# Two more column groups of a modulation product (3 and 4 of layer 1) summed on VectorE instead of on TensorE

## The chip, the core and the metric

The kernel runs on one core of a Trainium2 chip. The metric is the device time of one execution in microseconds (us), here the median of three runs. A profiled execution gives the trace that the rows below are read from; its times count from the start of its span.

## The reference, cut to what matters

Two layers work on 256 latent and 256 context tokens of width 2048. In each layer the conditioning vectors give a shift, a scale and a gate for every channel, which is a product of a small matrix (2 rows: latent and context) with a weight matrix of 2048 x 6144:

```
cond_x = silu(c); cond_c = silu(c_ctx)
sh, sc, gt = split(cond @ ada_w[i] + ada_b[i], 3)
u = modulate(rms_norm(h, pre_g[i]), sh, sc)
out = mixer_i(u)          # layer 0: convolution and Fourier; layer 1: attention and state space
h = h + gt * rms_norm(out, post_g[i])
```

All arithmetic is fp32. The modulation of layer 1 depends on the inputs alone, so it can be computed at any time before the input of layer 1 is formed.

## The kernel before

**Weights.** Every weight block of a projection is 512 KB: 2 x 128 rows by 512 columns. `load_w` fetches it into a tile with the tag raw (4 buffers) and splits it into wh (rounded, ScalarE, L73) and wl (the rest, VectorE, L76), of which there are 3 buffers each. Each product is then three matmuls. `next_w` keeps three blocks ahead (`fill_w(3)`, L313 is its DMA).

**Groups and turns.** `group` runs over the 8 weight blocks of a projection. After each block it calls a step function, here called a turn, which hands small pieces of other work to the scheduler at this place of the program. In layer 0 the groups with turns are, in order: five input groups of 8 turns (convolution values and gates, Fourier inputs), the Fourier gates 0 to 3 (8), the Fourier gates 4 to 7 (8), one convolution gate block alone (`nb=1`, `step_odd`: 4 turns in 8 weight blocks, which are 128 KB each here), the last convolution gates (8), and three of the four column blocks of the output product (8 each). That makes 92 turns. The fourth column block runs in two halves (`ao`), each followed by `mid_chain`, which ends layer 0 and gives the input of layer 1. `u1_pair` then forms that input, two channel blocks at a time, with the modulation.

**The modulation in the background.** It is cut into 12 column groups q of 512 columns for each layer; q of 0 to 7 hold scale and shift. Layer 0's first eight are done in a prologue, and the gates of layer 1 elsewhere. The others are done in the turns, by two queues:

- `ada_bg` holds `ada_steps`: per group 8 loads of 512 KB into raw (L359), 16 matmuls of the conditioning with the raw tile into E (L143, four at a time), a copy, and four transposes (ept, L128). It is eight steps per group, and one step is taken in every turn.
- `pool_bg` holds `ada_vec`: per group 8 loads of 512 KB into raw (L381), each with two row blocks of 128. For both conditioning vectors each row block is scaled and added to a sum pa: the first on ScalarE (L385), all others on VectorE (L387). At the end two matmuls with ones add up the partitions (Ep, L392), and four transposes bring the result into place (ept, L399). Each load is one step and the sum is the ninth; the finish falls into the step after it. The two sums have one buffer each.

`pool_bg` is stepped in two turns of three, and only from the moment that the sixth group is through:

```
def step_ada():
    turns[0] += 1
    if turns[1] and turns[0] % 3 < 2:
        run(pool_bg)
    run(ada_bg)
```

What is left of both queues after the third column block of the output product is issued at once, before the fourth:

```
pump(1e9)
run(ada_bg, 1e9)
run(pool_bg, 1e9)
out0_open(3)
```

**Order.** The program is ordered by a scheduler that goes by program order among what is ready on each engine. Engines run their instructions in the order that it fixed. SyncE issues all loads.

Of the kernel before, what the change touches and what calls it, by code (L numbers as in the profile page):

```python
# [40 lines left out]
def tile_backbone(ctx: ExitStack, tc: tile.TileContext, a):  # L41
# [77 lines left out]
    def ada_copy(E):  # L119
        es = scr.tile([P, 512], F32, tag="t512", name="es")  # L120
        S.activation(es, E, AF.Copy)
        return es

    def ada_finish(psp, l, q, es, tag="ps"):

        pt = psp.tile([P, 4, P], F32, tag=tag, name="ept")
        for b in range(4):
            T.transpose(pt[:, b, :], es[:, b * P:(b + 1) * P], ident)  # L128
        V.tensor_reduce(
            ada[l][:, 4 * q:4 * q + 4, :],  # L130
            pt.rearrange("p b (g m) -> p b m g", g=4)[:, :, 0:2, :],
            axis=AX.X, op=ALU.add,
        )
        lo = COLS["adab"][0] + 48 * l + 4 * q
        V.tensor_tensor(
            ada[l][:, 4 * q:4 * q + 4, :], ada[l][:, 4 * q:4 * q + 4, :],
            cols[:, lo:lo + 4].rearrange("p (b o) -> p b o", o=1).to_broadcast([P, 4, 2]),
            ALU.add,
        )

    def ada_mm(E, kt, raw):
        g = kt % 4
        T.matmul(E[32 * g:32 * g + 32, :], condS[:, kt, :], raw,  # L143
                 start=(kt < 4), stop=(kt >= 12), skip_group_check=True)
# [207 lines left out]
    def ada_steps(l, qs):  # L352
        for q in qs:
            E = epool[0].tile([P, 512], F32, tag=epool[1], name="E")
            for kq in range(4):
                ws = []
                for i in range(2):
                    w = wpool.tile([P, 2, 512], F32, tag="raw", name="raw", bufs=4)
                    nc.sync.dma_start(w, a["ada%d" % l][q, kq][:, 2 * i:2 * i + 2, :])  # L359
                    ws.append(w)  # L360
                    if i == 0:
                        yield
                for j in range(4):
                    ada_mm(E, 4 * kq + j, ws[j // 2][:, j % 2, :])
                if kq < 3:
                    yield
            es = ada_copy(E)
            yield
            ada_finish(epool[0], l, q, es, epool[1])
            ada_done(l, (q,))  # L370

    def ada_vec(l, qs, nm, pool):

        accs = []
        for i, q in enumerate(qs):
            accs += [pool.tile([P, 512], F32, tag="pa%d" % (i * nm + m), name="pa")
                     for m in range(nm)]
            for kp in range(8):
                w = wpool.tile([P, 2, 512], F32, tag="raw", name="raw", bufs=4)
                k0 = 2 * (kp % 2)  # L380
                nc.sync.dma_start(w, a["ada%d" % l][q, kp // 2][:, k0:k0 + 2, :])  # L381
                for kt, m in ((2 * kp + j, m) for j in range(2) for m in range(nm)):
                    acc, wj, c = accs[i * nm + m], w[:, kt % 2, :], condS[:, kt, m:m + 1]
                    if kt == 0:
                        S.activation(acc, wj, AF.Copy, scale=c)  # L385
                    else:
                        V.scalar_tensor_tensor(acc, wj, c, acc, ALU.mult, ALU.add)  # L387
                yield
        n = 32 * len(accs)
        E = psp.tile([P, 512], F32, tag="ps", name="Ep")  # L390
        for g, acc in enumerate(accs):
            T.matmul(E[32 * g:32 * g + 32, :], ones[:, 0:32], acc, start=True, stop=True,  # L392
                     skip_group_check=True)
        es = scr.tile([P, 512], F32, tag="t512", name="es")
        S.activation(es[0:n], E[0:n], AF.Copy)
        yield
        pt = psp.tile([P, 4, n], F32, tag="ps", name="ept")
        for b in range(4):
            T.transpose(pt[:, b, :], es[0:n, b * P:(b + 1) * P], ident[0:n, 0:n])  # L399
        for i, q in enumerate(qs):  # L400
            lo = COLS["adab"][0] + 48 * l + 4 * q
            V.tensor_tensor(
                ada[l][:, 4 * q:4 * q + 4, 0:nm],
                pt.rearrange("p b (q m r) -> p q r b m", q=len(qs), m=nm)[:, i, 0],
                cols[:, lo:lo + 4].rearrange("p (b o) -> p b o", o=1).to_broadcast([P, 4, nm]),
                ALU.add)
        ada_done(l, qs)
# [34 lines left out]
    def ada_done(l, qs):  # L442
        for q in qs:
            if q < 8:
                mod_cols(l, q)
            else:
                gates[l] += 1
                if gates[l] == 4:
                    gate_rows(l, *epool)
                    cond_row(*epool)  # L450
# [9 lines left out]
    ada_bg, pool_bg = [], []  # L460
# [49 lines left out]
    l0 = lay0.enter_context(tc.tile_pool(name="l0", side="right", reuse_waits="tile", bufs=1))  # L510
# [260 lines left out]
    utok = lambda kt, t: (uh[kt][:, t * P:(t + 1) * P], ul[kt][:, t * P:(t + 1) * P])  # L771
    kts = list(range(KT))
    for l, qs in ((0, range(8, 12)), (1, range(8))):
        ada_bg.append(ada_steps(l, [q for q in qs if (l, q) not in ((1, 5), (1, 6), (1, 7))]))
        pool_bg += [ada_vec(l, (q,), 2, l0) for q in qs if (l, q) in ((1, 5), (1, 6), (1, 7))]

    def step0():
        step_ada()
# [547 lines left out]
    qs = P ** -0.5  # L1326
# [233 lines left out]
```

## Time and profile before

| what | value |
|---|---|
| median of 3 runs | 1532.35 us (1530.88 to 1534.11) |
| profiled execution | 1529.52 us, of which its span is 1527.5 us |
| TensorE busy | 1467.2 us (96%) |
| VectorE busy | 1041.7 us (68%) |
| ScalarE busy | 568.2 us (37%) |
| mean granted clock of TensorE | 0.993 |

PE is TensorE's matmuls, PEld its weight loads, DVE VectorE, ACT ScalarE and SPq SyncE's queue of DMAs. L76 is line 76 of the kernel. A row of a timeline has the start, the duration, the engine, the line, the operation, output and inputs, the count of merged instructions, and in brackets the idle time before with what ended it.

### The profile page before, as it was taken

How to read it: one execution, taken by the hardware profiler on the slowest of the kernel's cores; microseconds unless marked ns; L12 is line 12 of the kernel's file. 1: busy time of each engine (PE TensorE's matmuls, PEld its weight loads, DVE VectorE, ACT ScalarE, POOL GpSimd, SP SyncE). 2: the span in 40 equal slices, each digit the busy share in tenths (PEclk: the TensorE clock that was granted, in tenths of full speed). 3: DMA queues.
4: the chain of work that ended last, by engine and by line, in shares of the span. 5: the costliest groups of instructions: out<-in, count | busy, mean ns of one | idle time of the engine just before them, and what ended most of it. 6: DMA issues, size and time to landing. Idle time of an engine off the chain costs nothing.

```text
span 1527.5 us, 22085 instructions
## 1 busy us (share of the span) xinstructions
PE 1467.2 (96%) x8261; PEld 1186.9 (78%) x8261; DVE 1041.7 (68%) x2427; ACT 568.2 (37%) x1113; POOL 183.6 (12%) x179
## 2 busy tenths in 40 slices
PE   3999999999999999999998999999999999999996
PEld 1556777777777766778778999897888979889885
DVE  5234999999863654655367725779799897746645
ACT  4232111122223323232256624454554545324542
POOL 0000000010130000000000100335144354000000
PEclk9999999999999999999999999999999999999998
DMA  9975444454615566664364534224344544536653
GB/s 387 365 307 226 143 164 166 164 168 142 207 45 186 204 207 221 204 204 160 103 223 170 169 108 145 83 101 149 132 160 133 176 143 145 201 117 209 227 189 114
DMA packets 75261, 269.89 MB, mean 177 GB/s; under 512 B 8401, under 2 KB 12049, under 8 KB 70417
## 3 DMA queue, kind: packets, MB, share of 16 engines
q1 hardware_dynamic: 75152, 268.47, 51.1%
q8 instruction: 65, 1.06, 0.3%
q14 instruction: 44, 0.35, 0.1%
HBM read 264.21 MB, written 4.23 MB: 176 GB/s over the span
## 4 chain that ended last, share of the span: by engine, by line
PE 79%; DVE 15%; DMA 3%; issue 2%; ACT 1%; SPq 0%; DVEq 0%; ACTq 0%
PE acc L495 35%; PE kv L495 12%; PE ao L495 8%; PE E L143 4%; DVE wl L76 3%; PE aq L495 2%; PE ag L495 2%; PE acc L204 2%; PE acc L205 2%; PE adg L495 1%; PE acc L203 1%; DMA raw<-in_ada1g_dram 1%; PE po L1296 1%; PE Sc L1267 1%; DVE acc L245 1%
## 5 line engine op out<-in xcount | busy, mean ns | idle before, releaser
L73 ACT ACTIVATE wh<-raw 128x1024 fp32r<-128x1024 f32 (+1 forms) x264 | 274.4, 1040 | 600.4 <-PE acc L495 267.8
L76 DVE TENSOR_TENSOR wl<-raw,wh 128x1024 fp32r<-128x1024 f32 (+1 forms) x264 | 322.4, 1224 | 202.9 <-ACT wh L73 202.0
L530 DVE SCALAR_TENSOR_TENSOR cv<-ain,cw,cv 128x512 f32<-128x512 f32 x240 | 170.4, 750 | 0.0
L495 PE MATMUL acc<-uh,wh 128*128 128x512 f32 x400 | 161.7, 404 | 2.5 <-ACT wh L73 2.0
L495 PE MATMUL acc<-uh,wl 128*128 128x512 f32 x400 | 158.0, 399 | 2.0 <-DVE wl L76 2.0
L495 PE MATMUL acc<-ul,wh 128*128 128x512 f32 x400 | 158.5, 396 | 0.0
L495 PE MATMUL kv<-wh,uh 128*128 128x256 f32 x384 | 109.8, 286 | 2.5 <-DVE sg L1341 2.5
L387 DVE SCALAR_TENSOR_TENSOR pa<-raw,condS,pa 128x512 f32<-128x512 f32 x90 | 63.1, 747 | 69.3 <-DMA raw<-in_ada_dram 62.6
L495 PE MATMUL kv<-wl,uh 128*128 128x256 f32 x384 | 109.4, 285 | 0.0
L495 PE MATMUL kv<-wh,ul 128*128 128x256 f32 x384 | 108.6, 283 | 0.0
L495 PEld LDWEIGHTS acc<-uh,wh 128*128 128x128 f32 x400 | 75.6, 189 | 41.5 <-ACT wh L73 11.0
L495 PEld LDWEIGHTS acc<-uh,wl 128*128 128x128 f32 x400 | 75.9, 190 | 22.2 <-DVE wl L76 2.8
L495 PE MATMUL kv<-uh,wh 128*128 128x512 f32 (+1 forms) x224 | 86.4, 388 | 5.9 <-ACT uh L920 5.9
L495 PEld LDWEIGHTS acc<-ul,wh 128*128 128x128 f32 x400 | 75.6, 189 | 17.0 <-issue 0.8
L495 PE MATMUL kv<-ul,wh 128*128 128x512 f32 (+1 forms) x224 | 82.7, 370 | 0.0
L495 PE MATMUL kv<-uh,wl 128*128 128x512 f32 (+1 forms) x224 | 82.2, 369 | 0.0
L495 PEld LDWEIGHTS kv<-wh,uh 128*128 128x128 f32 x384 | 72.7, 189 | 6.2 <-DVE sg L1341 3.4
L495 PE MATMUL acc<-wh,uh 128*128 128x512 f32 x192 | 76.7, 401 | 0.0
L495 PE MATMUL acc<-wl,uh 128*128 128x512 f32 x192 | 76.6, 399 | 0.0
L495 PE MATMUL acc<-wh,ul 128*128 128x512 f32 x192 | 76.3, 397 | 0.0
L495 PE MATMUL acc<-wh,mh 128*128 128x512 f32 x192 | 76.0, 398 | 0.0
L495 PE MATMUL acc<-wl,mh 128*128 128x512 f32 x192 | 75.5, 393 | 0.0
(405 smaller groups left out, 3328.1 us busy)
## 6 DMA issues: line engine op xcount, KB each, us to landing
raw<-in_w_dram SPq DMA_DIRECT2D x184, 512.0 KB, 3.5
raw<-in_ada_dram SPq DMA_DIRECT2D x96, 512.0 KB, 4.7
raw<-in_wo_dram SPq DMA_DIRECT2D x72, 512.0 KB, 3.2
aw<-in_ada_dram SPq DMA_DIRECT2D x32, 1024.0 KB, 7.1
raw<-in_ada1g_dram SPq DMA_DIRECT2D x32, 512.0 KB, 3.3
w<-in_w0a_dram SPq DMA_DIRECT2D x8, 896.0 KB, 6.8
h<-in_h_dram SPq DMA_DIRECT2D x4, 1024.0 KB, 8.0
h0t<-in_h0t_dram SPq DMA_DIRECT2D x16, 256.0 KB, 4.3
```

Source lines behind the costliest of these rows:

```text
L73: S.activation(hi, src, AF.Copy)
L76: slo.tensor_tensor(lo, src, hi.bitcast(F32), ALU.subtract)
L143: T.matmul(E[32 * g:32 * g + 32, :], condS[:, kt, :], raw, start=(kt < 4), stop=(kt >= 12), skip_group_check=True)
L203: T.matmul(ps, wh, xh, start=start, stop=False)
L204: T.matmul(ps, wh, xl, start=False, stop=False)
L205: T.matmul(ps, wl, xh, start=False, stop=stop)
L245: V.tensor_tensor(acc, acc, sq, ALU.add)
L387: V.scalar_tensor_tensor(acc, wj, c, acc, ALU.mult, ALU.add)
L495: T.matmul(out, lt, rt, start=st and m == 0, stop=en and m == 2, skip_group_check=True)
L530: ins = V.scalar_tensor_tensor(o, x[:, :, k:k + L], cw05[:, ch, k:k + 1], o, ALU.mult, ALU.add)
L1267: T.matmul(Sc, qT[:, i, t * P:(t + 1) * P], kT[:, i, :], start=True, stop=True)
L1296: T.matmul(po, vT[:, k, i * P:(i + 1) * P], U_["PT"][:, k, :], start=k == 0, stop=k == 3)
```

## The change

Column groups 3 and 4 of layer 1 are taken from the list of `ada_steps` and put into that of `ada_vec`, ahead of groups 5, 6 and 7, which were there before. Nothing else changes.

```diff
 for l, qs in ((0, range(8, 12)), (1, range(8))):
-    ada_bg.append(ada_steps(l, [q for q in qs if (l, q) not in ((1, 5), (1, 6), (1, 7))]))
-    pool_bg += [ada_vec(l, (q,), 2, l0) for q in qs if (l, q) in ((1, 5), (1, 6), (1, 7))]
+    ada_bg.append(ada_steps(l, [q for q in qs if (l, q) not in ((1, 3), (1, 4), (1, 5), (1, 6), (1, 7))]))
+    pool_bg += [ada_vec(l, (q,), 2, l0) for q in qs if (l, q) in ((1, 3), (1, 4), (1, 5), (1, 6), (1, 7))]
```

## Rows read from the trace of the kernel before

**Rows 1.** The page: busy time of each engine, share, instructions.

```profile
PE 1467.2 (96%) x8261; PEld 1186.9 (78%) x8261; DVE 1041.7 (68%) x2427; ACT 568.2 (37%) x1113; POOL 183.6 (12%) x179
```

**Rows 2.** Waits of TensorE, 480 to 840 us: total, times, longest.

```profile
PE kv L495 <- ACT uh L920: 5.9, 1, 5.9
PE acc L495 <- ACT wh L73: 2.0, 3, 1.0
```

**Rows 3.** The chain that ended last, 600 to 770 us: start, us, what.

```profile
607.35 0.99 PE E L143 x8
...
644.23 1.14 PE E L143 x8
...
651.14 0.51 PE ept L128 x4
...
736.58 0.98 PE Ep L392 x4
...
748.92 0.39 PE ept L399 x4
749.31 11.36 PE acc L495 x48
```

**Rows 4.** Timeline of SyncE's DMA queue, 480 to 840 us.

```profile
482.11 0.80 SPq L855 DMA_DIRECT2D h0t<-in_h0t_dram  x2
...
645.89 0.33 SPq L313 DMA_DIRECT2D raw<-in_wo_dram  x1
647.02 0.33 SPq L381 DMA_DIRECT2D raw<-in_ada_dram  x1
647.44 8.75 SPq L313 DMA_DIRECT2D raw<-in_wo_dram  x3
657.19 0.33 SPq L381 DMA_DIRECT2D raw<-in_ada_dram  x1
...
713.23 0.33 SPq L381 DMA_DIRECT2D raw<-in_ada_dram  x1
```

**Rows 5.** Busy time by window, the group of one block.

```profile
core 0: us, PE busy (x) PEld busy (x) DVE busy (x) ACT busy (x) POOL busy (x), PEclk, DMA share, GB/s
549.30:566.60 17.30, 15.26 (x62) 9.01 (x60) 7.56 (x16) 4.57 (x10) 0.00 (x0) 1.00 0.71 229
```

**Rows 6.** Busy time by window of the instructions on E alone.

```profile
549.30:566.60 17.30, 3.16 (x12) 0.43 (x12) 0.00 (x0) 1.00 0.71 229
570.00:760.00 190.00, 8.71 (x52) 1.43 (x52) 1.16 (x2) 1.00 0.55 181
```

**Rows 7.** The chain that ended last, 545 to 570 us.

```profile
549.20 5.01 DMA raw<-in_w0t_dram
```

**Rows 8.** Tile pa: ns (min/median/max), first and last start.

```profile
L387 DVE SCALAR_TENSOR_TENSOR pa<-raw,condS,pa x90: 740/746/754, 490.1 to 720.5; 128x512 f32<-128x512 f32 x90
...
L385 ACT ACTIVATE pa<-raw,condS x6: 708/718/726, 489.3 to 664.9; 128x512 f32<-128x512 f32 x6
```

**Rows 9.** Timeline of VectorE, 640 to 665 us.

```profile
643.12 2.74 DVE L387 SCALAR_TENSOR_TENSOR pa<-raw,condS,pa 128x512 f32<-128x512 f32 x4 [4.55 <-DMA raw<-in_ada_dram]
```

**Rows 10.** Timeline of VectorE, 715 to 832 us.

```profile
726.55 1.23 DVE L76 TENSOR_TENSOR wl<-raw,wh 128x1024 fp32r<-128x1024 f32 x1 [1.73 <-ACT wh L73]
...
737.71 1.23 DVE L76 TENSOR_TENSOR wl<-raw,wh 128x1024 fp32r<-128x1024 f32 x1 [4.34 <-ACT wh L73]
744.47 1.23 DVE L76 TENSOR_TENSOR wl<-raw,wh 128x1024 fp32r<-128x1024 f32 x1 [5.54 <-ACT wh L73]
...
750.05 1.23 DVE L76 TENSOR_TENSOR wl<-raw,wh 128x1024 fp32r<-128x1024 f32 x1 [0.34 <-ACT wh L73]
...
761.49 0.69 DVE L874 TENSOR_TENSOR oG<-acc,gt 128x512 f32<-128x512 f32 x1 [0.77 <-ACT jk L873]
```

**Rows 11.** DMA issues, 700 to 790 us: count, size, median us to landing.

```profile
raw<-in_wo_dram SPq DMA_DIRECT2D x22, 512.0 KB, 3.2
raw<-in_ada_dram SPq DMA_DIRECT2D x2, 512.0 KB, 4.4
```

**Rows 12.** Busy time by window after the wait in the middle.

```profile
819.50:825.00 5.50, 5.36 (x24) 5.34 (x25) 4.33 (x16) 5.50 (x16) 0.00 (x0) 0.50 0.01 5
```

## The prediction, written before the change was run

> **What bounds the kernel now.** I read the shares of the engines first: TensorE is busy 96% of the span [rows 1]. Then who waited for whom on TensorE around the stretch that the change touches, 480 to 840 us: its two longest waits add up to 7.9 us, one of 5.9 us behind the middle chain and 2.0 us in three pieces [rows 2]. So in this stretch TensorE sets the time, and any TensorE work taken out is won, as long as nothing new makes it wait. Third, the chain that ended last, 600 to 770 us: it is an unbroken run of TensorE work, in which the summed modulation appears as blocks of 1 us (E, and ept behind it) between weight products [rows 3]. VectorE is not the bound here, but it shares one thing with TensorE's supply: the four buffers with the tag raw. Every weight block of `load_w` and every modulation block passes through them, and SyncE issues them in the order of the program [rows 4].
>
> **What is removed.** Groups 3 and 4 leave `ada_steps`. Each is 16 matmuls, four at a time, and four transposes. On the chain four matmuls take 0.99 to 1.14 us and the transposes 0.51 us [rows 3]. Two groups: 8 x 1.02 + 2 x 0.5 = about 9 us. This counts them as they overlap on the chain; the busy time of all records of the two groups, 3.16 + 8.71 us [rows 6], holds their tails too and is the upper bound, 12. The Trainium skill (TensorE: Matmul & The Clock Gate, "Part 3: Packing small matmuls — row/col tiling") says the same: matmuls with 32 output rows that go to different column groups of the array run side by side, 2.38 times as fast for three of them. So this rule speaks against the change: what it takes away was already cheap. The trace agrees (four fp32 matmuls in 0.99 us); run one after another they would be, by the same row's factor as an estimate, some 20 us instead of 8, and the sum below would be +4 or +5.
>
> The two groups are also the last two of `ada_bg`. That queue gives one step per turn and eight steps per group, nine groups now, so it ends with turn 72; after the change with turn 56. Turns 57 to 60 are the group with one block (the gate of channel block 7), where each weight block carries only 6 matmuls; it lasts 17.3 us with TensorE busy 15.3 [rows 5], and the chain runs there through DMAs into raw buffers (5.0 us the first, [rows 7]). Four of the modulation loads vanish from it. I take the 2 us of idle time as won; bounds 0 and 2.7 (17.3 less its 48 products, which take 11.4 us [rows 3], and less 3.2 us of E [rows 6]).
>
> Gain together: 11 us (9 to 14.7).
>
> **What is added on VectorE, and when.** `ada_vec` costs per load of 512 KB four VectorE operations, 2.74 us in a row; the first load of a group has two of them on ScalarE at 0.72 us [rows 8, 9]. In sum 60 operations, 41 us. VectorE has that much idle time in the stretch; what decides is the moment. `pool_bg` is stepped only from turn 49 (the flag is set after six groups of eight turns) and only in turns whose number leaves 0 or 1 by three. The turns end at 92: six groups of 8, one of 8, four half turns, one of 8, three of 8. That is turn 49 and 14 pairs from 51 to 91: 29 steps. A group takes nine steps (eight loads, then the sum on TensorE), with the finish falling into the next. Three groups need 28: they just fit, and the last load of the trace at 713.23, the last sum at 736.58 and its transposes at 748.92 lie where turns 87, 88 and 90 are [rows 3, 4]. Five groups need 46. So groups 3, 4 and 5 take the places of 5, 6 and 7, group 6 gets its first two loads in turns 90 and 91, and **six loads of group 6 and all eight of group 7 are left for `run(pool_bg, 1e9)`**, between the third and the fourth column block of the output product. These 14 loads, 7.3 MB, stand in program order behind the first two weight blocks of the fourth column block (the prefetch of three) and ahead of its third.
>
> Does the issue order keep to that? From 645.89 to 657.19 the queue shows a weight and a modulation load, three weights and a modulation load: turns 73 to 76, of which 74 has no step and the step of 75 is a sum without a load [rows 4]. Loads into other free buffers are lifted far ahead (h0t at 482, [rows 4]), but the raw buffers always have an earlier load waiting. So I take strict order.
>
> **The new wait.** All times here are those of the profiled execution before; what TensorE gains moves both sides alike. A raw buffer comes free when the VectorE half of the split (wl) ends: 727.8, 738.9, 745.7, 751.3 [rows 10], with one more between the first two that the 25th weight block takes. The two loads of turns 90 and 91 take those of 727.8 and 738.9. The first can't be worked on until the sum of the group ahead of it has read pa (736.58+0.98), and ends at 740.4; that buffer goes to the 26th weight block. The first dumped load is then issued at 745.7 and with 4.4 us to landing [rows 11] is there at 750.1. Behind it three buffers turn into modulation loads as well, and from 751.3 on VectorE sets the pace. The third weight block (the 27th of the output product) needs the buffer of the 11th dumped load. Up to there VectorE has 42 operations of 0.685 us (2.74/4) = 28.8 us, one wl 1.2, four evacuations of 0.69 = 2.8 [rows 10], and between groups 6 and 7 the sum on TensorE and the two ScalarE copies, 2.4 us. 751.3 + 35.2 = 786.5. Then 3.2 us for the load [rows 11] and twice 1.2 for the halves of the split (wh taken as long as wl): 792. The fourth column block begins at 749.31 + 11.36 = 760.67, and each of its weight blocks feeds 12 products in a half, 2.8 us at 11.36 for 48 [rows 3]. So TensorE wants the third at 766.3. **TensorE stands still for about 25 us.** Behind VectorE's modulation work waits the wl of the weights, and behind that TensorE alone; nothing else is ready for it, because the fourth column block is the input of the middle norm.
>
> Bounds: if VectorE packs the 28.8 us and two wl without a gap from 746, the block is ready at 783 and the wait is 16; if its wl is queued behind the 14th load and the last sum stands ahead of the products on TensorE, 797 and 31. The sums and transposes of groups 6 and 7 on TensorE (2 x 1.37 us, [rows 3]) fall into this wait and cost nothing; without it they cost 2.7.
>
> After its 5.9 us wait in the middle, TensorE ran at a granted clock of 0.50, the lower level, for 5.5 us [rows 12], 2.7 us lost. After the new wait I take 2 us, since the next weight blocks come only every 2.8 us anyhow (bounds 0 and 3).
>
> **Sum.** -9 - 2 + 25 + 2 = +16 us; bounds -14.7 + 16 = +1 and -9 + 31 + 3 = +25. The profiled execution has 1529.52 us (span 1527.5 and 2.0 around it); the median of the runs is 2.8 above. On its own time 1545.5, on the runs' 1548.
>
> **Rivals.** *Order not kept (other sign):* the weight loads of the fourth column block are let through between the modulation loads, so that two loads of the group at a time reach VectorE. It then has 14 x 2.74 = 38 us to do in the 45 us from 740 to 785, of which 17 go to weights and evacuations; it runs on into the middle chain by some 10 us without holding back products much. -11 + 3 = 1524. For it: h0t lifted to 482 [rows 4], and VectorE idle between its wl [rows 10]. Against it: the order seen from 645 to 657. It decides if the 27th block is split before 777, that is, a wait under 11 us. Chance 0.11.
> *Half hidden:* the modulation loads get in earlier, in the buffers that the missing loads of turns 57 to 72 leave, and the wait is 9 to 14 us: 1530 to 1535, taken as 1532. Against it: a freed buffer goes to the next load in order, and that is a weight block which waits for its wh buffer. Chance 0.06.
> *Longer:* TensorE's queue has the last sum and transposes ahead of the products, and the loads of the rest of the column block come one by one: wait 35, clock 3: -9 + 38 = 1561. Chance 0.07.
> *No change from the edit:* excluded as to the sums; both groups do move.
> Forecast (wait 16 to 31): 0.76.
>
> **Numbers.** 0.2% (3 us) is about what runs can tell from no change. Faster by more: the first rival and a little of the second, 0.12. Within: most of the second, 0.05. Slower: 0.83. Range: from the forecast's lower end to its upper one, 1533 to 1557; the lowest needs the best end of every term at once, so 1535 to 1558; outside are the first rival and most of the two others, about 2 in 10.
>
> **What would show it.** No E blocks after some 545 us; the group of one block shorter by 3 to 5 us; the fourth column block begun some 10 us earlier, 14 modulation loads in a row on the queue before it, and one idle time of TensorE of 16 to 31 us behind wl two blocks into it. Wrong would be: weight loads between those 14; modulation operations on VectorE before 735 for groups 6 and 7; a TensorE wait elsewhere, as in turns 57 to 92, because VectorE's order puts wl behind operations that wait for DMA.

## The result, and the profile after

The changed kernel has a median of 1547.15 us (1543.42 to 1549.91, 4 runs); the kernel before has 1531.69 us (1530.88 to 1534.11) beside it. The ratio is 1.0091 [1.0072, 1.0109]: 15.5 us slower. The profiled execution has 1548.74 us with a span of 1546.8. It lies 1.6 above the median and that of before 2.2 below the median beside it, so two profiles differ by 19.3 us where the medians differ by 15.5; sizes below are taken stretch by stretch.

The page's busy times of the kernel after, which answer to [rows 1]:

```profile
PE 1464.5 (95%) x8205; PEld 1187.1 (77%) x8205; DVE 1078.1 (70%) x2485; ACT 570.8 (37%) x1117; POOL 182.7 (12%) x179
```

VectorE has 36.4 us more. TensorE has only 2.7 us less in a longer span: part of what it saved it gave back in matmuls that took longer. The waits of TensorE, 480 to 860 us, beside [rows 2]:

```profile
PE ao L495 <- ACT wh L73: 15.9, 1, 15.9
PE kv L495 <- ACT uh L920: 6.6, 1, 6.6
PE Ep L392 <- DVE pa L387: 3.4, 1, 3.4
```

The second is the wait in the middle chain that was there before (5.9). The first and the third are new, and `ao` says where: in the fourth column block of the output product. SyncE's queue of the kernel after, 710 to 830 us, beside [rows 4]:

```profile
727.54 0.33 SPq L381 DMA_DIRECT2D raw<-in_ada_dram  x1
728.87 0.33 SPq L313 DMA_DIRECT2D raw<-in_wo_dram  x1
734.45 38.06 SPq L381 DMA_DIRECT2D raw<-in_ada_dram  x14
774.83 33.13 SPq L313 DMA_DIRECT2D raw<-in_wo_dram  x14
```

Fourteen modulation loads (L381) stand in a row, and between 728.87 and 774.83, 46 us, no weight block (L313) is issued. VectorE of the kernel after, 720 to 790 us, with the work that goes with those loads, beside [rows 9, 10]:

```profile
753.64 6.05 DVE L387 SCALAR_TENSOR_TENSOR pa<-raw,condS,pa 128x512 f32<-128x512 f32 x9
...
765.45 13.99 DVE L387 SCALAR_TENSOR_TENSOR pa<-raw,condS,pa 128x512 f32<-128x512 f32 x21
779.36 1.22 DVE L76 TENSOR_TENSOR wl<-raw,wh 128x1024 fp32r<-128x1024 f32 x1
```

The operations stand back to back (21 in 13.99 us, 0.67 each, as 0.685 before), and the first wl of the late weight block comes behind them. TensorE of the kernel after, 745 to 803 us:

```profile
750.01 0.50 PE L495 MATMUL ao<-wh,mh 128*128 128x512 f32 x1 [0.76 <-DVE oG L874]
...
759.18 2.49 PE L392 MATMUL Ep<-pa,ones 128*32 128x512 f32 x4 [3.42 <-DVE pa L387]
762.40 0.68 PE L399 MATMUL ept<-ident,es 64*128 64x64 f32 x4 [0.74 <-ACT es L395]
778.99 1.22 PE L495 MATMUL ao<-wh,mh 128*128 128x512 f32 x2 [15.90 <-ACT wh L73]
...
786.00 1.05 PE L392 MATMUL Ep<-pa,ones 128*32 128x512 f32 x2
...
789.96 1.04 PE L392 MATMUL Ep<-pa,ones 128*32 128x512 f32 x2
```

The column block begins at 750.01. TensorE works off two weight blocks, does the sum of group 6 inside the idle time, and begins the third weight block at 778.99. The sum of group 7 stands among the products, in two parts, one for each conditioning vector. Windows of the kernel after over this place (columns as in [rows 5]):

```profile
749.60:755.80 6.20, 5.75 (x24) 4.43 (x24) 6.20 (x11) 0.43 (x2) 0.00 (x0) 1.00 0.57 182
755.80:779.00 23.20, 3.18 (x9) 0.88 (x9) 21.00 (x34) 2.92 (x4) 0.00 (x0) 0.56 0.56 183
779.00:786.00 7.00, 6.58 (x14) 4.29 (x14) 6.71 (x8) 2.43 (x3) 0.00 (x0) 0.51 0.79 287
786.00:803.00 17.00, 17.00 (x70) 12.04 (x70) 7.02 (x9) 6.73 (x9) 0.00 (x0) 1.00 0.57 186
```

VectorE is busy 21.0 of the 23.2 us in which TensorE gets no product. In the next 7.0 us the granted clock is 0.51, the lower level: 14 products (the 12 of a weight block and two of the next) need 7.0 us. At the 11.36 us for 48 of [rows 3] they would take 3.3.

**The bill.** I measure from the last evacuation of the third column block (the start of its last ScalarE copy) to that of the first half of the fourth: 760.77 to 782.91 before, 22.1 us; 749.35 to 802.53 after, 53.2 us. Of the 31 us more, 23.2 are the stretch without products, 3.7 the lower clock (7.0 less 3.3, 0.4 of it a wait for wl), and 2.6 the two parts of group 7's sum and its transposes inside the products (1.05 + 1.04 + 0.46, the last at 796.72); 1.5 us are left, 0.8 of them the wait for oG at the start.

### The profile page after: what moved, and what is told of

Its sections match the earlier page's. It is cut to its first block, busy times and chain, and to the rows that moved or that the text cites. A ratio compares the mean times of both kernels' runs of the same rounds, so it can differ in the third digit from the quotient of the medians.

```text
span 1546.8 us, 22054 instructions
## 1 busy us (share of the span) xinstructions
PE 1464.5 (95%) x8205; PEld 1187.1 (77%) x8205; DVE 1078.1 (70%) x2485; ACT 570.8 (37%) x1117; POOL 182.7 (12%) x179
## 3 DMA queue, kind: packets, MB, share of 16 engines
q8 instruction: 64, 1.05, 0.3%
## 4 chain that ended last, share of the span: by engine, by line
PE 74%; DVE 16%; DMA 5%; issue 2%; ACT 2%; SPq 0%; DVEq 0%; ACTq 0%
PE acc L495 29%; PE kv L495 13%; PE ao L495 8%; DVE wl L76 4%; PE E L143 4%; DMA raw<-in_ada_dram 3%; DVE pa L387 3%; PE aq L495 3%; PE ag L495 3%; PE acc L204 2%; PE acc L205 2%; PE adg L495 1%; PE acc L203 1%; PE po L1296 1%; DMA raw<-in_ada1g_dram 1%
## 5 line engine op out<-in xcount | busy, mean ns | idle before, releaser
L387 DVE SCALAR_TENSOR_TENSOR pa<-raw,condS,pa 128x512 f32<-128x512 f32 x150 | 104.4, 746 | 74.2 <-DMA raw<-in_ada_dram 65.1
```

## The experiments

Theory: the price is the 14 left-over loads in one piece, with VectorE's work on them setting the pace ahead of the third weight block; spread over the turns they would cost little. Rivals: the loads alone, through the shared buffers, hold the block up; or the work costs TensorE time wherever it is put. Ratios are over three rounds beside the kernel before on the same chip, with the median of the kernel ahead of them. Diffs are against the kernel after, if nothing else is said.

**1. A step in every turn.** More turns give a step, so that nothing is left over.

```diff
-        if turns[1] and turns[0] % 3 < 2:
+        if turns[1]:
```

> The VectorE queue of the changed kernel is stepped in every turn from turn 49 on, not in two of three. All five groups still go to VectorE, with the same operations and loads. Theory (the 14 loads that are issued in one piece ahead of the third weight block make TensorE stand still): 44 of the 46 steps find a turn, only the last sum and its finish are left over, the idle time is gone, and what remains is the TensorE work saved (some 11 us to the start of the fourth column block) less two sums of 1.4 us: 1522 to 1526 us, against 1531.7 before and 1547.2 after the change. Rival (41 us of VectorE work and 8 MB through the raw buffers cost as such, wherever they stand): 1540 to 1550.

1528.29 us; 0.9968 [0.9954, 0.9982], 2 us above the range that I had expected and far from the rival's. The 15.9 us wait is gone and the kernel is faster than both. But 10 us of the gain alone (experiment 3) are missing: the half of the fourth column block takes 26.7 us instead of 22.1, and the second column block 49.3, where before it took 44.9. Most of that can be read off: each of the two stretches holds the sum and the transposes of a group, which before has elsewhere (some 1.6 us: its third column block, with such a sum among its 192 products, takes 46.2 us, and at 22.29 us for 96 the products alone take 44.6), and each has two waits of TensorE, 1.3 and 1.0 us and 1.3 and 0.7 us. That makes 3.9 of 4.4 us and 3.6 of 4.6.

**2. Four groups instead of five.** Only group 4 moves, so 6 loads are left over instead of 14.

```diff
-    ada_bg.append(ada_steps(l, [q for q in qs if (l, q) not in ((1, 3), (1, 4), (1, 5), (1, 6), (1, 7))]))
-    pool_bg += [ada_vec(l, (q,), 2, l0) for q in qs if (l, q) in ((1, 3), (1, 4), (1, 5), (1, 6), (1, 7))]
+    ada_bg.append(ada_steps(l, [q for q in qs if (l, q) not in ((1, 4), (1, 5), (1, 6), (1, 7))]))
+    pool_bg += [ada_vec(l, (q,), 2, l0) for q in qs if (l, q) in ((1, 4), (1, 5), (1, 6), (1, 7))]
```

> Only group 4 is moved to VectorE besides 5, 6 and 7; group 3 stays on TensorE. Theory: 37 steps for 29 turns, so 6 loads are issued in one piece instead of 14. The third weight block then needs the buffer of the third of them, which is done about when TensorE comes to it: a wait of 0 to 6 us against a gain of 5: 1526 to 1533 us, that is, far less than half of the loss. Rival (cost goes with the VectorE work): half of the loss of two groups, 1539.

1531.82 us; 0.9994 [0.9983, 1.0004]: no difference from before, as expected. SyncE's queue of this kernel, 700 to 800 us:

```profile
741.05 14.54 SPq L381 DMA_DIRECT2D raw<-in_ada_dram  x6
```

The half takes 27.2 us, 5 more than before instead of 31. So the price hangs on how many loads are left over together with their work on VectorE, and with six of them it eats the gain of one group.

**3. The gain alone.** Groups 3 and 4 are left out on both engines; constants stand in for them.

```diff
+    G.memset(ada[1], 0.0)
...
+    G.memset(Am[1], 1.0)
...
-    pool_bg += [ada_vec(l, (q,), 2, l0) for q in qs if (l, q) in ((1, 3), (1, 4), (1, 5), (1, 6), (1, 7))]
+    pool_bg += [ada_vec(l, (q,), 2, l0) for q in qs if (l, q) in ((1, 5), (1, 6), (1, 7))]
```

> Groups 3 and 4 are left out altogether: on TensorE as in the changed kernel, and on VectorE too, so shift and scale of these 8 channel blocks are constants. Groups 5, 6 and 7 are as before the change. Theory: the gain by itself, 9 us of TensorE work and some 2 us of waiting in the group of one block: 1520 to 1523 us. Rival (the summed modulation on TensorE was hidden, or its loads did not hold anything up): 1526 to 1531.

1517.97 us; 0.9902 [0.9879, 0.9924]: 2 us below the range, a larger gain than expected. The half takes 22.1 us, as before. The gain is 14.4 us by the medians, and 12.8 by the start of the last evacuation of the third column block (747.99 against 760.77). By the ratios the price in the kernel after is 1.0091 - 0.9902 = 0.0189 of 1532, 29.0 us. By the two intervals such a price is uncertain by some 4 us, here and below. It holds the sums of two more groups on TensorE too, which this kernel leaves out.

**4. The left-over loads without most of their VectorE work.** In them each operation takes 32 of the 512 columns.

```diff
-    V.scalar_tensor_tensor(acc, wj, c, acc, ALU.mult, ALU.add)
+    n_ = 32 if dumped else 512
+    V.scalar_tensor_tensor(acc[:, 0:n_], wj[:, 0:n_], c, acc[:, 0:n_], ALU.mult, ALU.add)
...
+    dumped.append(1)
     run(pool_bg, 1e9)
```

> The changed kernel, but the operations on VectorE that belong to the 14 loads left over at the end take 32 of the 512 columns, so the sums of groups 6 and 7 are incomplete; the loads, their order and all buffers stay. Theory (VectorE sets the pace at which the buffers come free, 2.7 us per load): without it the 14 loads run at the pace of the transfers, 7.3 MB, and the wait shrinks from 23 us to 5 or 8: 1525 to 1531 us. Rival (the transfers themselves and their order set the pace): the wait stays at some 20 us, 1542 or more.

1535.54 us; 1.0013 [0.9998, 1.0027], a miss: the price falls by 12 us and not by nearly all. The queue in this kernel, and the sums of groups 6 and 7 on TensorE, the second with its longest wait:

```profile
734.50 25.67 SPq L381 DMA_DIRECT2D raw<-in_ada_dram  x14
```

```profile
754.26 1.05 PE L394 MATMUL Ep<-pa,ones 128*32 128x512 f32 x4
...
767.80 2.05 PE L394 MATMUL Ep<-pa,ones 128*32 128x512 f32 x4 [8.92 <-DVE pa L388]
```

The 14 loads go out in 25.67 us instead of 38.06, 1.8 us each. That is not nothing, and the wait has moved to the sum of group 7: TensorE has it ahead of the products of the third weight block, and it needs the last of the 14 loads. The sum of group 6 (754.26) has no wait any more.

**5. The loads alone.** As experiment 4, and the sums of groups 6 and 7 on TensorE left out as well, with constants in their place as in experiment 3.

```diff
+        if dumped:
+            return
```

> The changed kernel with the 14 left-over loads kept in their place and order, their VectorE operations cut to 32 columns, and without the two sums on TensorE at the end of groups 6 and 7 (the modulation of their channel blocks is constants). In the run with 32 columns TensorE waited 8.9 us in a sum that stood ahead of the weight products until the last load had landed. Theory (loads cost the transfer pace, 1.8 us each, and the rest of that run's loss was the place of the sums): 1536 - 9 - 3 = 1522 to 1527 us. Rival (the order of the loads holds back the third weight block whatever follows them): stays at 1532 to 1536.

1532.43 us; 0.9996 [0.9983, 1.0009]: the rival's range. TensorE's longest wait in this kernel, and the queue:

```profile
PE ao L502 <- ACT wh L73: 11.0, 1, 11.0
```

```profile
730.10 24.80 SPq L383 DMA_DIRECT2D raw<-in_ada_dram  x14
```

With little work on VectorE behind them, the 14 loads ahead of it still hold up the third weight block. Price: 0.9996 - 0.9902, 14.4 us. Whether the four buffers, the order in the queue or the pace of the transfers does it is not separated by this run.

**6. The VectorE work alone.** The left-over loads are omitted, and their operations read a constant tile.

```diff
-    w = wpool.tile([P, 2, 512], F32, tag="raw", name="raw", bufs=4)
...
-    nc.sync.dma_start(w, a["ada%d" % l][q, kp // 2][:, k0:k0 + 2, :])
+    if not dumped:
+        w = wpool.tile([P, 2, 512], F32, tag="raw", name="raw", bufs=4)
...
+        nc.sync.dma_start(w, a["ada%d" % l][q, kp // 2][:, k0:k0 + 2, :])
...
+        wj = ident.rearrange("p (o q) -> p o q", o=1).to_broadcast([P, 4, P])
```

> The changed kernel without the 14 left-over loads: their 56 operations run all the same, in the same place of the program, on a constant tile that is always there, and the sums on TensorE follow. Theory A (the operations must pass through the raw buffers, and the weights wait for these): without the loads nothing holds back the third weight block, 1520 to 1527 us. Theory B (VectorE takes what is ready in program order, so 38 us of its work stand ahead of the wl of the third weight block, with or without loads): the idle time remains, starting a little earlier: 1540 to 1546.

1533.53 us; 0.9999 [0.9984, 1.0014]: between the two expectations. Its waits of TensorE, 480 to 860 us:

```profile
PE z L918 <- DVE dg L908: 14.4, 1, 14.4
PE Ep L398 <- DVE pa L393: 3.2, 1, 3.2
```

No wait stands ahead of the third weight block. VectorE takes wl and modulation in turns, and the loss comes to rest in the middle chain instead. ScalarE, 792 to 800 us, has the reason:

```profile
798.76 0.59 ACT L401 ACTIVATE es<-Ep 64x512 f32<-64x512 f32 x1 [5.19 <-PE Ep L398]
799.25 0.58 ACT L880 ACTIVATE jk<-ao 128x512 f32<-128x512 f32 x1
```

The evacuation of the first half (jk) stands in ScalarE's fixed order behind the copy of group 7's sum (es), and that waits for the sum, which waits for VectorE. So the half is evacuated at 799.25, when TensorE is through with the second half too (its last product starts at 792.1), and the middle chain of the first half has no products left to cover it: the 14.4 us. Price 14.9 us, by another wait than in the kernel after. Loads alone (14.4) and work alone (14.9) add up to 29.3, and the whole is 29.0; as the waits are different ones, and each price is uncertain by some 4 us, this sum does not share the price out.

**7 and 8. A buffer of their own.** One of the four raw buffers goes to the loads of `ada_vec` (the diff shows these); at every other place that loads into raw, `bufs` becomes 3. 7 is the kernel after with it, 8 the kernel before.

```diff
-                w = wpool.tile([P, 2, 512], F32, tag="raw", name="raw", bufs=4)
+                w = wpool.tile([P, 2, 512], F32, tag="praw", name="praw", bufs=1)
```

> The changed kernel with the four buffers raw divided: three for the weights and TensorE's modulation, one of its own for the loads of the VectorE groups. Turns, queues and all operations as in the changed kernel, 14 loads still issued last in the program. Theory (the shared buffers bind these loads to their place in the program): with a buffer of their own they are lifted ahead, VectorE does them in its idle time at one per some 7 us, no standstill before the third weight block: 1520 to 1530 us, unless three buffers starve the weights, which the next run tells. Rival (VectorE is too late with 41 us more work whatever the order): 1540 or more.

> The kernel before with the same division of the buffers, three and one: what the division costs or brings by itself with three groups on VectorE. Expected 1528 to 1536 us (the same within 0.3%), since the weights hold a buffer for some 5 us of the 5.6 us that a block lasts. The difference to the run before is the effect of the two groups when order is no matter: theory -8 to -12 us, rival +10 or more.

1576.36 us, 1.0291 [1.0255, 1.0327], and 1552.70 us, 1.0121 [1.0092, 1.015]. The first fell in the range of its rival, the second missed. Tile pa in 7, two issues of its loads on SyncE's queue, and the waits of TensorE:

```profile
L387 DVE SCALAR_TENSOR_TENSOR pa<-praw,condS,pa x150: 742/746/753, 154.4 to 838.1; 128x512 f32<-128x512 f32 x150
...
L392 PE MATMUL Ep<-pa,ones x20: 592/617/1061, 557.5 to 839.8; 128*32 128x512 f32 x20
```

```profile
233.43 0.33 SPq L381 DMA_DIRECT2D praw<-in_ada_dram  x1
...
561.46 0.33 SPq L381 DMA_DIRECT2D praw<-in_ada_dram  x1
```

```profile
PE Ep L392 <- DVE pa L387: 20.3, 1, 20.3
PE z L911 <- DVE dg L901: 14.1, 1, 14.1
```

VectorE's operations begin at 154 us instead of 490, and still end at 838. Nine loads go out by 233.43, and the tenth only at 561.46: the ninth is the first of group 4, and can't be worked on until TensorE has read group 3's sum out of pa, which has one buffer; the first sum on TensorE stands at 557.5. From 674.71 to 720.21 none goes out again, until the sum of group 5 at 715.9. Otherwise a load follows every 6 to 10 us from 561 on, because with one buffer landing and VectorE's work follow each other, and the end is that of experiment 6: the evacuation of the first half (841.36) behind the copy of group 7's sum (840.86). The division costs 20 us by itself (8), so the pair does not tell what sharing the buffers costs. It does show that starting early is no help when the sum's own buffer, and each load, must wait for the one before.

**9 and 10. Spreading the steps.** Both aim at leaving next to nothing for the end. 9 gives a step in every turn after turn 60:

```diff
-        if turns[1] and turns[0] % 3 < 2:
+        if turns[1] and (turns[0] > 60 or turns[0] % 3 < 2):
```

10 starts at turn 41 as well:

```diff
-        if turns[1] and turns[0] % 3 < 2:
+        if turns[0] > 60 or (turns[0] > 40 and turns[0] % 3 < 2):
```

> Five groups on VectorE; two turns of three up to turn 60 as in the changed kernel, every turn from 61 on, when the loads for TensorE's modulation have ended. 40 of 46 steps find a turn, four loads and the last sum are left over. Theory (only what is left over in one piece costs): with four loads the third weight block finds its buffer in time; two sums of 1.4 us in the way of TensorE and little else: 1531.9 - 14.4 (measured without the groups) + 2.8 + 0 to 4, that is 1520 to 1525 us. Rival (more loads per turn hold back the weights as in the run with every turn): 1526 to 1530.

> As the run before, but the two turns of three begin with turn 41 and not 49: 45 of 46 steps find a turn, only the finish of the last group is left over. Theory: no load is left over, but turns 41 to 48 have a third load per turn beside the weights and TensorE's modulation: 1520 to 1524 us if that costs nothing, and 1524 to 1528 if it costs what turns 49 to 60 cost in the run with every turn (about 3 to 5 us).

1535.39 us, 1.0013 [0.9996, 1.003], and 1525.74 us, 0.9951 [0.9937, 0.9966]. The second beats both kernels (7 us below before, 21 below after), in the upper one of its two ranges, and lies 7.5 us above the gain alone, of which the sums of two more groups are some 3; the first missed, and is not to be told from before.

**11 and 12. Four groups, spread.** Groups 4 to 7 are on VectorE, as in experiment 2. 11 has a step for each of the 37 that four groups need:

```diff
-        if turns[1] and turns[0] % 3 < 2:
+        if turns[0] > 60 and turns[0] % 4 < 3 or (40 < turns[0] <= 60 and turns[0] % 3 < 2):
```

12 has 34 of them:

```diff
-        if turns[1] and turns[0] % 3 < 2:
+        if turns[0] > 40 and turns[0] % 3 < 2:
```

> Four groups on VectorE (group 3 back on TensorE), with exactly as many steps as they need: two turns of three from 41 to 60, three of four from 61 on, 37 in all, so nothing is left over. Theory: half of the 14 us that leaving out two groups gave, less one sum of 1.6 us and some 2 to 4 us for the loads in turns 41 to 48: 1527 to 1531 us, between the kernel before and the one with five groups spread. Rival (fewer groups leave the weights more room, so that the whole gain of the group arrives): 1524 to 1526.

> Four groups on VectorE again, now in two turns of three from turn 41 to the end: 34 steps for the 37 they need, so one load, a sum and a finish are left over. In the run with three turns of four a weight load stood 32 us in all (8 times) behind a modulation load that had not landed yet, and a column block took 51 to 52 us; with two of three it took 45 in the changed kernel. Theory (the turn without a modulation load lets VectorE and the buffers catch up): 45 to 47 us for a column block, one left-over load costs nothing, 1524 to 1529 us. Rival (what the two runs differ in is how the scheduler happened to place the loads, not the rate): 1532 or more, with column blocks of 48 us and over.

1542.69 us, 1.0065 [1.0045, 1.0085], and 1540.59 us, 1.0040 [1.0027, 1.0053]. 11 missed, and 12 went to the rival. By then my theory, that only what is left over in one piece costs, had fallen: 9, 11 and 12 have few or no loads left over, and 9 gains nothing, 11 and 12 lose. Their traces show where. The time from one column block's last evacuation to the next, in us:

| kernel | to the 2nd | to the 3rd | half of the 4th |
|---|---|---|---|
| before | 44.9 | 46.2 | 22.1 |
| after | 44.9 | 47.9 | 53.2 |
| 9, every turn after 60 | 53.9 | 51.5 | 26.8 |
| 10, started at 41 | 46.2 | 48.1 | 23.9 |
| 11, four groups | 51.1 | 52.2 | 22.7 |
| 12, four groups | 54.1 | 44.4 | 24.0 |

The long ones begin with a wait for the evacuation. TensorE's longest waits in 9 and in 12, 480 to 860 us, first:

```profile
PE acc L495 <- DVE oG L874: 8.5, 2, 5.1
```

```profile
PE acc L495 <- DVE oG L874: 5.0, 1, 5.0
```

VectorE in 9 and in 12, 655 to 685 us, has the reason:

```profile
661.06 1.41 DVE L387 SCALAR_TENSOR_TENSOR pa<-raw,condS,pa 128x512 f32<-128x512 f32 x2 [2.78 <-DMA raw<-in_ada_dram]
662.39 1.22 DVE L76 TENSOR_TENSOR wl<-raw,wh 128x1024 fp32r<-128x1024 f32 x1
663.53 0.74 DVE L387 SCALAR_TENSOR_TENSOR pa<-raw,condS,pa 128x512 f32<-128x512 f32 x1
664.19 0.68 DVE L874 TENSOR_TENSOR oG<-acc,gt 128x512 f32<-128x512 f32 x1
```

```profile
667.95 2.08 DVE L387 SCALAR_TENSOR_TENSOR pa<-raw,condS,pa 128x512 f32<-128x512 f32 x3 [4.89 <-DMA raw<-in_ada_dram]
669.94 1.22 DVE L76 TENSOR_TENSOR wl<-raw,wh 128x1024 fp32r<-128x1024 f32 x1
671.08 0.74 DVE L387 SCALAR_TENSOR_TENSOR pa<-raw,condS,pa 128x512 f32<-128x512 f32 x1
671.74 2.48 DVE L874 TENSOR_TENSOR oG<-acc,gt 128x512 f32<-128x512 f32 x4
```

The evacuation (oG) has to clear the accumulators before the next column block can begin. The last of its four ScalarE copies starts at 659.89 in 9 and at 667.53 in 12, so the products are through by then; the first of the VectorE operations follows only at 664.19 and 671.74, because it stands in the fixed order behind modulation operations of which the first is idle for its DMA. In 10 the first runs at 664.24, before the last copy starts (664.71), and TensorE waits 0.4 us there. After the wait comes the lower clock, in 9:

```profile
665.00:672.00 7.00, 7.00 (x21) 5.55 (x22) 6.20 (x9) 0.00 (x0) 0.00 (x0) 0.65 0.76 242
```

At 0.65 over 7.0 us about 2.4 us are lost. With the 5.1 us of the wait that is 7.5 of the 9 us by which this column block is longer than in before; a group's sum, some 1.6 us, stands in it as well, and before has none there. In 11 the waits of this stretch (oG 5.3, Ep 2.0, wl 1.3 us) cover 8.6 of the 12 us that its two long blocks lose. The place of the loss is so shown. That it would go with the evacuations put ahead of the modulation in VectorE's order was not tried.

## Why the prediction was right, and where not

**Direction, place and mechanism held.** The last E record begins at 549.8 us; the group of one block takes 12.6 us instead of 17.3, in the 3 to 5 us that I had named; 14 modulation loads go out in a row, with no weight load among them; the wait stands two weight blocks into the fourth column block, and nothing covers it. The count of steps (46 for 29 turns) gave the right number of left-over loads, and experiment 2, with 6 of them, came out in the expected range. The order was kept, so the first rival did not occur, and neither did the other two.

**The moment was right to 2.5 us.** I had the third weight block ready at 792 in the frame of before. The column block began 10.5 us earlier than in before (750.0 against 760.5; predicted 11), so 792 becomes 781.5; measured, the first product starts at 778.99. VectorE did set the pace, at 0.67 us per operation against my 0.685. Experiments 4 to 6 put a limit to that term: VectorE's work was not the whole price. Without most of it the loads alone still cost 14.4 us, which my reckoning of operation times did not hold apart.

**The term of the wait.** Predicted 25, bounds 16 to 31. The stretch without products is 23.2 us. Here the prediction was right, by its own steps.

**Terms that were mis-sized.** *Lower clock:* 2 us, bounds 0 to 3; measured 3.7, or 3.3 without the wait for wl, outside the bounds. I had taken the next weight blocks to come too slowly for the clock to matter, but the products of the late block itself ran one after another at 0.43 us (785.06 less 781.22 for nine), so the clock counted in full. *Sums in the wait cost nothing:* true of group 6, whose sum lies in the idle time; not of group 7, whose sum stands among the products and costs 2.6 us, where I had named 2.7 for both groups without cover. Its two matmuls stand apart and take 1.05 and 1.04 us, as long each as both together in before (0.98). *Gain:* 11, bounds 9 to 14.7; measured 13.7 in the trace of the kernel after, counted as in the next paragraph, and 14.4 by the medians of experiment 3.

**Why the gain was larger.** The mis-sized term is "8 x 1.02": I counted blocks of four matmuls, at the time that their own rows show. First the measure. The 12.8 us of experiment 3 compares two clocks that differ: the group of one block begins at 549.34 in before, at 551.66 in the kernel after and at 550.94 in experiment 3, and the first two are 2.3 us apart from 201 us on (201.15 against 203.50 for the same E record), long before the edit has an effect. Counted from the start of this group, the last evacuation of the third column block comes 13.7 us earlier in the kernel after and 14.4 in experiment 3. The group itself in the kernel after, beside [rows 5]:

```profile
551.60:564.20 12.60, 11.76 (x51) 8.88 (x48) 8.02 (x18) 4.64 (x11) 0.00 (x0) 1.00 0.60 172
```

It is 4.7 us shorter: three places of E, and 1.1 us of waiting less (0.42, 0.98 and 0.63 in before; 0.40 and 0.48 in after), where I had taken 2 for the waiting. Then the places of E. Each of these matmuls has two records (the trace of the kernel after has 64 fewer on E, for 32 matmuls). In before, the 64 records of groups 3 and 4 stand not in eight places but in eleven, since the order has split three of the blocks of four, and half a block takes as long as a whole one. TensorE in before, 545 to 600 us:

```profile
562.31 1.05 PE L143 MATMUL E<-raw,condS 128*32 128x512 f32 x4
...
594.49 1.07 PE L143 MATMUL E<-raw,condS 128*32 128x512 f32 x8
```

Last, what a place costs. In the kernel after, the chain that ended last, 500 to 860 us, shows two of them among products of layer 0, and an unbroken run:

```profile
499.87 12.05 PE acc L495 x51
511.92 0.98 PE E L143 x4
512.91 10.66 PE acc L495 x45
523.57 0.98 PE E L143 x4
...
582.81 66.88 PE acc L495 x288
```

The 96 products and two places of E take 24.68 us (524.55 less 499.87). In the unbroken run 96 products take 22.29. So a place costs 1.2 us, of which its own row shows 0.98; the rest is in the products around it. Eleven places at 1.2, two rows of transposes at 0.5 and 1.1 us of waiting make 15.3 us. The third column block takes back 0.9 us of it in experiment 3 (47.1 us instead of 46.2) and 1.7 in the kernel after (47.9), most of it in a wait for the evacuation at its start (0.5 and 1.2 us). That leaves 14.4 and 13.6, as measured.

The Trainium skill (TensorE: Matmul & The Clock Gate, "Part 3: Packing small matmuls — row/col tiling") has such narrow matmuls run side by side, and I cited it against the change. The rows agree again: two matmuls in 1.05 us and four in 1.07 by the rows above, and one alone in 1.05 in group 7's sum. What their place among full products costs beyond that, the 0.2 us, came from the chain alone.

**Two errors of opposite sign.** Gain 14.4 instead of 11, price 29 instead of 27. That the predicted 1548 lies so near the measured 1547.15 is luck: it is closer than the terms were.

**What stays open.** Which schedule falls well was not to be foretold: 10, with 45 of its 46 steps in the turns, loses 7.5 us to the gain alone; 11, with all of its 37, loses far more. The wait of the evacuation behind a DMA shows where the difference arises. Why the order falls out so in one and not in the other is the scheduler's doing, and no run separates it. What in experiment 5 lets the loads alone hold up the weight block, the buffers, the queue or the transfers, was not separated either.

## What to carry to other kernels

Before moving work to an idle engine, count the places that will issue it against the steps it needs: what doesn't fit comes in one piece, and if its loads share buffers and a queue with the weights, they hold up the weights even where the engine has time. Then ask where each moved operation lands in the fixed order of its new engine: an operation that waits ahead of an evacuation, for a DMA on VectorE (9, 12) or for a sum on ScalarE (6, 7), stops TensorE, however small its work is. When narrow matmuls are taken out, count the places in which they stand, not the matmuls. Spreading the steps from earlier on got half of the gain here (1525.74 us against 1532.50), and it must be tried on the chip, since a schedule that looks alike lost it.

## What the runs showed of the hardware that was not expected

One, two or four narrow matmuls in one place took the same time (1.05, 1.05 and 1.07 us by their rows), and a place of two among full products cost about 1.2 us on the chain, though its own row there gives 0.98. After a wait of TensorE the granted clock stays low well into the work: 0.51 for the 7.0 us after the new wait, in which 14 products took 7.0 us instead of 3.3; and inside the wait a sum (two matmuls, four records) took 2.49 us, where 0.98 had been its price before. In experiment 9 it was low after a wait of 5.1 us too, 0.65 on the mean of 7.0 us. In these two places a wait of TensorE cost its own length and 2 to 4 us more.
